# Tree-masked attention: stores moved from SyncE's hardware queue to GpSimd's software queue, behind the loads, with ten output buffers

## The chip, the cores and the metric

One NeuronCore of a Trainium2 chip. The metric is the device time of one execution in microseconds, median of several runs; lower is better. The profile's span is some 1.5 us shorter than that time. Engines are PE (TensorE), DVE (VectorE), ACT (ScalarE), POOL (GpSimd) and SP (SyncE). Sixteen DMA engines move the data, whichever of them issues it.

## The reference

Attention over 8 batches and 12 heads, 512 positions of 64 numbers, where a position sees only itself and its ancestors in a binary tree:

```python
mask[i, i] = 1
parent = i
while parent > 0:
    parent = (parent - 1) // 2
    mask[i, parent] = 1
scores = np.einsum('bhqd,bhkd->bhqk', Q, K) / np.sqrt(dim)
scores = scores + (1 - mask) * (-1e9)
weights = np.exp(scores - np.max(scores, axis=-1, keepdims=True))
weights = weights / (np.sum(weights, axis=-1, keepdims=True) + 1e-10)
return np.einsum('bhqk,bhkd->bhqd', weights, V)
```

Q, K, V and the result are 12.6 MB each in fp32: 37.7 MB are read, 12.6 MB written.

## The kernel before

It works on 48 pairs of heads, i = 0 to 47, six to a batch. For each: transposes of Q and K on PE (`tq`, `tk`), copies to `qt` (DVE) and `kt` (ACT), scores (`st`, `stx`), exponentials on ACT, values into `o`, then a reciprocal and a multiplication on DVE into `of`, which is stored. DVE also spreads each batch's V into `v` and `vx` ("copies"). The parts that matter:

```python
opool = ctx.enter_context(tc.tile_pool(name="opool", bufs=4))     # rec and of
...
def load(upto):                       # all loads that are due up to pair `upto`
    while plan and plan[-1][0] <= upto:
        _, src, b, h0, h1 = plan.pop()
        ...                           # 6 buffers each for Q, K and V of a batch
        nc.gpsimd.dma_start(          # fp32 -> bf16 on the way
            out=loaded[kind, b][:, h0:h1, :],
            in_=src[b, h0:h1].rearrange("h (p t) d -> p h (t d)", t=T),
        )
...
def values(i):
    ...
    nc.vector.tensor_tensor(out=of4, in0=o4[:, :, :, 0:D], in1=..., op=ALU.mult)
    nc.sync.dma_start(                # 128 partitions x 2 heads x 1 KB
        out=out[b, 2 * hp:2 * hp + 2].rearrange("h (p t) d -> p h (t d)", t=T),
        in_=of[:, :, :],
    )
...
for i in range(N):
    load(i + 9)
    if i + 2 < N:
        transposes(i + 2)
    if i + 1 < N:
        scores(i + 1)
    values(i)
    ...                               # a few of the copies of V
```

The order on PE, DVE, ACT and GpSimd is the program's order. DMAs issued on GpSimd share eight completion semaphores in turn, so each waits for the eighth before it.

The softmax here doesn't subtract the row's maximum and nothing guards it: scores larger than these inputs give would overflow.

## Time and profile before

| | before |
|---|---|
| time, median | 157.4 us |
| span in the profile | 156.0 us |
| busy: PE, DVE, ACT, POOL | 120, 103, 111, 49 us |
| loads on q0 / stores on q1 | 18.9 MB (bf16 side) / 12.6 MB and 0.5 MB of constants |

No compute engine is busy over 77% of the span, while the DMA engines are full until about 136 us. The prediction below shows the slices, the chain and the DMA queues, and reads them.

### The profile page before, as it was taken

The page shows a single profiled execution, that of the slowest core. Times are in us where ns is not written, and L with a number is a line of the kernel's source. Part 1 is how long each engine was busy: PE and PEld are TensorE (multiplying, and loading weights), DVE is VectorE, ACT ScalarE, POOL GpSimd, SP SyncE. Part 2 cuts the span into 40 slices and gives each one's busy share as a digit, 9 for nine tenths or more (in the row PEclk, how much of TensorE's full clock was granted, in tenths as well). Part 3 has the DMA queues.
Part 4 walks back from the last instruction along what each step waited for, and adds up shares of the span by engine and source line. Part 5 has one row for each costly group of instructions (what it writes and reads, how often), then busy time and mean ns, then how long its engine had stood idle before and what let it go on. Part 6 is the DMA issues. An engine that isn't in the chain of part 4 may idle for free.

```text
span 156.0 us, 5918 instructions
## 1 busy us (share of the span) xinstructions
PE 120.0 (77%) x2592; PEld 86.2 (55%) x2592; DVE 102.8 (66%) x243; ACT 111.0 (71%) x145; POOL 48.8 (31%) x65
## 2 busy tenths in 40 slices
PE   0539983966989897786998949986998659989950
PEld 0226752644667675564676627664676426767740
DVE  2119798097499876975589664986699635696541
ACT  3145792565799996985598937996899816999950
POOL 7974712333441323403432143503341130000000
PEclk9999999597799999999699977999999965999996
DMA  4999999999999999999999999999999999933432
GB/s 139 154 187 196 193 215 239 226 200 220 219 226 240 235 233 241 225 237 227 222 221 237 234 235 226 215 236 238 227 227 235 243 227 215 211 113 132 138 113 93
DMA packets 51210, 32.33 MB, mean 207 GB/s; under 512 B 1776, under 2 KB 51056, under 8 KB 51184
## 3 DMA queue, kind: packets, MB, share of 16 engines
q0 software_dynamic: 37840, 18.88, 89.6%
q1 hardware_dynamic: 13344, 13.08, 29.3%
q8 instruction: 20, 0.33, 0.8%
q14 instruction: 6, 0.05, 0.1%
HBM read 38.24 MB, written 12.58 MB: 326 GB/s over the span
## 4 chain that ended last, share of the span: by engine, by line
DMA 78%; PE 8%; DVE 4%; issue 3%; ACT 3%; POOL 2%; POOLq 0%
DMA ks<-in_K_dram 40%; DMA qs<-in_Q_dram 23%; DMA vs<-in_V_dram 15%; PE o L358 3%; DVE of L367 2%; PE st L311 2%; ACT etx L335 2%; PE stx L311 1%; POOL qs L222 1%; PE tk L275 1%; ACT kt L298 1%; PE tq L275 1%; DVE vx L261 1%; DVE rec L364 1%; ACT et L324 1%
## 5 line engine op out<-in xcount | busy, mean ns | idle before, releaser
L298 ACT COPY kt<-tk 128x512 bf16<-128x512 bf16 x48 | 28.2, 587 | 34.5 <-PE tk L275 33.9
L324 ACT ACTIVATE et<-st 128x1024 bf16<-128x1024 f32 x48 | 49.2, 1024 | 4.0 <-PE st L311 3.5
L358 PE MATMUL o<-v,et 128*64 128x65 bf16 (+1 forms) x576 | 39.0, 204 | 6.1 <-DVE v L261 4.8
L335 ACT ACTIVATE etx<-stx 128x768 bf16<-128x768 f32 x48 | 38.6, 804 | 0.0
L358 PE MATMUL o<-vx,etx 128*64 128x65 bf16 (+1 forms) x576 | 37.8, 200 | 0.8 <-issue 0.8
L358 PEld LDWEIGHTS <-et 128*64 128x64 bf16 (+1 forms) x576 | 28.9, 110 | 13.6 <-DVE v L261 5.9
L367 DVE TENSOR_TENSOR of<-o,rec 128x512 f32<-128x512 f32 x48 | 33.2, 691 | 1.7
L275 PE MATMUL tq<-ptile,qs 128*64 128x128 bf16 x384 | 21.6, 237 | 15.6 <-DMA qs<-in_Q_dram 10.1
L364 DVE RECIPROCAL rec<-o 128x8 f32<-128x8 f32 x48 | 9.8, 205 | 35.7 <-PE o L358 35.5
L222 POOL DMA_DIRECT2D qs<-in_Q_dram x26 | 20.3, 780 | 41.8 <-DMA vs<-in_V_dram 25.9
L358 PEld LDWEIGHTS <-etx 128*64 128x64 bf16 (+1 forms) x576 | 30.0, 111 | 0.4 <-issue 0.4
L261 DVE COPY vx<-vs 32x1536 bf16<-32x1536 bf16 (+3 forms) x54 | 28.8, 533 | 1.2
L222 POOL DMA_DIRECT2D ks<-in_K_dram x26 | 19.5, 750 | 30.7 <-DMA qs<-in_Q_dram 20.4
L275 PE MATMUL tk<-ptile,ks 128*64 128x128 bf16 x384 | 21.6, 238 | 8.4 <-DMA ks<-in_K_dram 8.1
L297 DVE COPY qt<-tq 128x512 bf16<-128x512 bf16 x48 | 19.9, 414 | 9.8 <-PE tq L275 9.3
L311 PEld LDWEIGHTS <-kt 64*128 64x128 bf16 x480 | 19.9, 102 | 11.4 <-issue 4.2
L275 PEld LDWEIGHTS <-qs 128*64 128x64 bf16 x384 | 15.2, 116 | 17.3 <-DMA qs<-in_Q_dram 10.6
L275 PEld LDWEIGHTS <-ks 128*64 128x64 bf16 x384 | 15.6, 121 | 10.7 <-DMA ks<-in_K_dram 9.4
L311 PE MATMUL st<-ctile 64*128 64x512 bf16 x96 | 20.3, 419 | 0.1
L311 PE MATMUL st<-qt,kt 64*128 64x512 bf16 x96 | 20.2, 417 | 0.1
L311 PE MATMUL stx<-qt,kt 64*128 64x96 bf16 x384 | 17.7, 215 | 0.5 <-issue 0.5
L311 PE MATMUL stx<-ctile 64*128 64x384 bf16 x96 | 17.3, 356 | 0.1
(11 smaller groups left out, 35.7 us busy)
## 6 DMA issues: line engine op xcount, KB each, us to landing
out_dram<-of SPq DMA_DIRECT2D x48, 256.0 KB, 6.2
qs<-in_Q_dram POOLq DMA_DIRECT2D x22, 256.0 KB, 19.1
ks<-in_K_dram POOLq DMA_DIRECT2D x22, 256.0 KB, 18.7
vs<-in_V_dram POOLq DMA_DIRECT2D x7, 768.0 KB, 22.4
vs<-in_V_dram POOLq DMA_DIRECT2D x2, 384.0 KB, 7.3
qs<-in_Q_dram POOLq DMA_DIRECT2D x4, 128.0 KB, 10.4
ks<-in_K_dram POOLq DMA_DIRECT2D x4, 128.0 KB, 10.0
ctile<-tree_codes SPq DMA_DIRECT2D x1, 288.0 KB, 3.1
```

The source lines that it names most:

```text
L222: nc.gpsimd.dma_start(out=loaded[kind, b][:, h0:h1, :], in_=src[b, h0:h1].rearrange("h (p t) d -> p h (t d)", t=T),)
L261: nc.vector.tensor_copy(out=o, in_=i)
L275: nc.tensor.matmul(out=o[D * hi:D * hi + D], rhs=perms[mat], lhsT=src[:, 2 * hp + hi, D * t:D * t + D], start=True, stop=True, is_transpos ...
L297: nc.vector.tensor_copy(out=qt[:, :], in_=tq[:, :])
L298: nc.scalar.copy(out=kt[:, :].rearrange("d (i j x) -> d i j x", j=2, x=32), in_=tk[:, :].rearrange("d (j i x) -> d i j x", j=2, x=32)[:, 0:8],
L311: nc.tensor.matmul(out=dst, lhsT=lhsT, rhs=rhs, start=first, stop=True, skip_group_check=not first,)
L324: nc.scalar.activation(out=et1[:, :, :], in_=st1[:, :, :], func=AF.Exp, scale=scale)
L335: nc.scalar.activation(out=etx[:, :, :, 32:P], in_=stx[:, :, 0:384].rearrange("p h (c q) -> p h c q", c=T), func=AF.Exp, scale=scale,)
L358: nc.tensor.matmul(out=o2[p0:p1, hi, (D + 1) * t:(D + 1) * (t + 1)], lhsT=e, rhs=v, start=kind == 0, stop=kind == 1,)
L364: nc.vector.reciprocal(out=rec[:, :, :, :], in_=o4[:, :, :, D:D + 1])
L367: nc.vector.tensor_tensor(out=of4, in0=o4[:, :, :, 0:D], in1=rec[:, :, :, :].to_broadcast([P, 2, T, D]), op=ALU.mult,)
```

## The change

Its intent: loads set the pace, and a store on a queue of its own takes its turns from them at once. Issued on GpSimd, behind the loads due nine pairs ahead, stores wait in the same ring until those loads have gone. Outputs then live longer, hence ten buffers. The last three stores have no load behind them and stay on SyncE.

```diff
-    opool = ctx.enter_context(tc.tile_pool(name="opool", bufs=4))
+    opool = ctx.enter_context(tc.tile_pool(name="opool", bufs=10))
...
-    state = {}
+    state, done = {}, {}
...
-        nc.sync.dma_start(
+        done[i] = of
+
+    def store(i):
+        b, hp = pairs[i]
+        eng = nc.gpsimd if i < N - 3 else nc.sync
+        eng.dma_start(
             out=out[b, 2 * hp:2 * hp + 2].rearrange(
                 "h (p t) d -> p h (t d)", t=T
             ),
-            in_=of[:, :, :],
+            in_=done.pop(i)[:, :, :],
         )
...
             load(i + 9)
+            if 0 < i < N - 2:
+                store(i - 1)
             if i + 2 < N:
                 transposes(i + 2)
             if i + 1 < N:
                 scores(i + 1)
             values(i)
+            if i >= N - 3:
+                store(i)
```

## The prediction

> **What bounds the kernel now.** I read the page's slices first, then the chain of work that ended last, then the waits, then the DMA view cut to stretches. The chain, first as shares of the span on the page, then as pieces in order of time (start, length, what):
>
> ```profile
> DMA 78%; PE 8%; DVE 4%; issue 3%; ACT 3%; POOL 2%; POOLq 0%
> ```
>
> ```profile
> 88.20 19.07 DMA qs<-in_Q_dram
> 107.28 0.28 issue
> 107.56 19.55 DMA ks<-in_K_dram
> 127.12 0.04 issue
> 127.16 0.64 PE tk L275 x8
> ```
>
> For 127 of 156 us the end hangs on one load behind another; from then on the chain is compute to the end. The load that hands over is K of heads 8 to 11 of batch 6. The first pair that needs it is pair 40 (pairs are counted 0 to 47), and its transposes are the ones at 127.16. The timeline of TensorE and VectorE shows that the last `of` of pair 47 ends at 152.66, so ten pairs' results (38 to 47) come in the 25.5 us after that landing: at first at half clock (the view of stretches has 0.50 for 127 to 133 us), later at 2.16 us a pair. This tail is compute, and the loads are ahead of it: the trace's last load lands at about 138 us, and pair 47's transposes are at 145.6.
>
> The page's slices and the DMA view say what the loads wait for. Whole span first, then 8 to 17 us (no store yet), 47 to 97 us (steady), and 0 to 125 us. Columns: packets, MB, time of the packets as a share of 16 engines.
>
> ```profile
> DMA  4999999999999999999999999999999999933432
> ```
>
> ```profile
> q0 software_dynamic: 3468, 1.72, 143.1%
> ```
>
> ```profile
> q0 software_dynamic: 13159, 6.57, 96.6%
> q1 hardware_dynamic: 5095, 4.91, 36.1%
> ```
>
> ```profile
> q0 software_dynamic: 34640, 17.31, 102.6%
> q1 hardware_dynamic: 10054, 9.91, 28.9%
> ```
>
> The engines are busy from 4 us to about 136 us. q0 carries the casting loads (1 KB fp32 in, 512 B bf16 out), q1 the stores (1 KB each). With the stores taken out, loads alone go at one packet per 42.9 ns and engine: 8 to 17 us is 9 us x 16 engines = 144 us of engine time for 1.72 MB / 512 B = 3,360 load packets. From 47 to 97 us there are 800 us of engine time for 6.57 MB / 512 B = 12,830 loads and 4.91 MB / 1,024 B = 4,795 stores; 12,830 x 42.9 ns = 550 us, the other 250 us are the stores': 52 ns each. A store of one head pair (256 KB, 16 packets per engine) thus costs 0.83 us of all 16 engines.
>
> **Does that add up to 127?** Before K of pair 40, each engine carries Q and K of 7 batches and V of 8: 14 x 96 + 8 x 96 = 2,112 packets, 17.30 MB in all; the view of 0 to 125 us has 17.31 MB, so the data are through at 125 and land 2 us later. 2,112 x 42.9 ns = 90.6 us. Stores by then: 9.91 MB less 0.49 MB of constants, 35.9 stores, x 0.83 us = 29.9 us. With 2.8 us until the first load has been issued and 2 us for landing the sum is 125.3; 1.8 us are left for the slow start and the constants. So the landing of that K, which sets the end, contains about 30 us of stores.
>
> **What the Trainium skill says.**
> - "DMA: Bandwidth & Descriptors", section "Queues, rings and completion order": each DMA engine takes turns between the queues that have work, and within a queue descriptors are taken in order. The trace agrees: a store issued on SyncE lands in a median of 6.2 us while loads issued before it take about 19 us, so a store on its own queue overtakes them.
> - Same page, "Anatomy of one DMA — SWDGE (gpsimd) path": the completion increment waits until the last byte is confirmed, longest for HBM, though the write of the semaphore itself is a tiny bubble. In the trace before, stores have their own queue, so whether such a completion holds up loads behind it in the same ring isn't shown.
> - "Advanced Engine Details and Errata", section "Clock Domains": an unobstructed 1 KiB descriptor takes 42 to 43 ns. The 42.9 ns of the loads agree with that; the 52 ns of the mixed stores lie above it.
> - "SBUF — State Buffer", section "SBUF: two separate sides": a DMA issued from GpSimd can starve for descriptors while VectorE holds the shared port in a fast mode. In the trace most descriptor runs are 0.70 to 0.85 us whatever VectorE does, the longest 1.22 us, so I give this little weight.
>
> **The change part by part.** The instruction order of the changed kernel shows PE, DVE and ACT unchanged; 45 store issues move from SyncE into GpSimd's stream, 3 stay.
>
> *What it reorders.* On GpSimd, store i-1 stands behind the loads due at iteration i, which run 9 pairs ahead. In one ring that is also the order of the transfers. Ahead of K of pair 40 stand stores 0 to 27, 28 of them, where the kernel before had moved 35.9. The total of bytes is the same; 7.9 stores go from before the landing that counts to after it.
> - At the old cost: 7.9 x 0.83 = 6.6 us earlier.
> - If a store packet in the same ring costs 47 ns, which is what store packets take when they have the engines alone (143 to 155 us: 37.5% of 12 us x 16 engines for 1.57 MB / 1,024 B = 1,533 packets): 28 x 16 x 47 ns = 21.1 us in place of 29.9, so 8.8 us earlier.
> - If it costs what a load costs, 42.9 ns: 19.2 us, so 10.7 us earlier.
> I take 8.8 us, because taking turns between two queues is the one thing that the mixed stretch has and the others don't, but I can't show that the 5 ns come from it.
>
> *What it costs GpSimd.* 45 more issues of about 0.75 us (the page's rows L222: 751 and 742 ns in the median) are 34 us on an engine that is busy 49 of 156 us. Per batch it issues 7 loads and 6 stores in 6 pairs x 2.7 us = 16 us, 1.25 us apiece. Beside the path.
>
> *What it adds as waits.* A GpSimd DMA reuses the semaphore of the eighth before it, so 8 are in flight: now some 4 loads and 4 stores (about 10 us of transfers) where it was 8 loads (19 us). A store also waits for its `of`. By the eighth-before rule, store 29 comes up when Q of pairs 38 and 39 has landed; compute is then near pair 34. So it has been ready for some 5 pairs, and the stream shouldn't stand.
>
> *The ten buffers.* `of` of pair j needs store j-10 landed. That store is right behind the loads of pair j+2 (for j = 6b+1, behind the next V as well), while `of` of j comes after the transposes of pair j+2 on PE anyway, about 3.7 us after their load's landing (127.1 to 130.8 in the chain). A store's 0.8 us and 2 us of landing fit in; behind a V (96 packets x 42.9 ns = 4.1 us) up to 2 us of wait may show, in a place where the next K isn't there yet.
>
> *Does the gain reach the end?* K of pair 40 lands at 127.1 - 8.8 = 118.3. The loads after it are 192 packets per engine (8.2 us) and 7 stores (5.3 us): the last lands at about 132, and pair 47 needs some 7 us more: 139. The compute tail from pair 40 ends at 118.3 + 25.5 = 143.8, so it still sets the end. The stores left at 132 are 13 x 0.75 = 10 us, done as their data come; the last is on SyncE, as before. Then 3.3 us from the last `of` to the end of the span, as before: span 147.2, and with the 1.35 us between the profile's span and the median time, **148.5 us**.
>
> **Rivals.**
> - *Store completions stall the ring.* If the increment after a write to HBM holds up the next load's data by 0.3 us or more, 28 stores cost 8.4 us and the gain is gone; at 0.5 us the kernel gets slower. For: stores that end alone take at least 2.1 us from issue to landing, for 0.75 us of data. Against: completion packets take 9 to 22 ns on either queue in the trace. It would make 155 to 162.
> - *GpSimd stands on a store whose pair isn't computed, and loads behind it come late.* Against: 5 pairs of slack above. For: the slack is counted on landings, and a slow stretch of compute would eat it. Some 150 to 153.
> - *One ring is better than two by more than the packets' time.* Then stores cost 43 ns or less, K of pair 40 lands at 116 and the time is 145 to 147. Compute stops it from going much lower: 48 pairs at some 2.35 us with spreading and a start of 15 us make an estimate of 128 to 130, plus the end.
> - *The time was hidden anyway* (compute the bound throughout). Against: the chain, and 34 us of idle ScalarE before its copy of K, released by `tk`. It would make 157.
>
> **Range and chances.** The sums at the three packet costs give 151, 148.5 and 146.5; waits move it up, a better ring down. Range 143.5 to 155. Faster by over 2% (under 154.2) needs only a third of the reckoned gain, so 0.77; within 2%, 0.16; slower, for a ring that stalls on completions, 0.07.
>
> **What would show it.** Right: the chain still hands over from a load of K to PE, at about 118 us; 28 stores, not 36, moved by then; the tail after it 25 us; DMA full to about 134 us with a higher sum in its last slices; loads land in some 10 us from issue, stores on GpSimd likewise; GpSimd's waits for VectorE near zero before the last loads. Wrong: long waits of GpSimd on `of`; VectorE idle before its multiplication, released by a store; slices of DMA below 9 in the middle; a rate per packet above 52 ns for stores. A chain that is PE, ACT or DVE from well before 110 us would mean that I have mistaken the bound after the change.

## The result, and the profile after

144.0 us in the median of four runs (143.25 to 145.38), against 157.37: the ratio is 0.916, with a 95% interval of 0.909 to 0.924. Ratios here are the mean time of one kernel's runs over that of the other's runs of the same rounds, so not quite the ratio of the medians quoted. Executions over 1.5% slower than the fastest of the same kernel are left out of the means. The result is correct. The time lies in the stated range, near its lower end; the gain is 13.4 us where 8.9 were reckoned.

The slices of the page of the changed kernel, in 40 parts of the span:

```profile
DMA  4999999999999999999999999999999999998343
GB/s 136 150 184 191 195 200 195 199 197 205 267 238 234 274 271 239 219 246 261 267 235 237 269 265 244 222 249 264 267 225 233 267 257 265 260 320 312 136 145 103
```

The DMA engines are as full as before. Until the tenth slice (35 us) there are almost only loads, near 197 GB/s; from then on, until about 124 us, 219 to 275 GB/s, where the kernel before had about 232 on average in its steady stretch. So it isn't only the order: in the same time more is moved. The same stretch as the prediction's, 47 to 97 us, from the DMA view of the changed kernel:

```profile
DMA packets 16163, 12.56 MB, mean 251 GB/s; under 512 B 662, under 2 KB 14907, under 8 KB 16151
q0 software_dynamic: 16151, 12.39, 134.0%
```

Loads (512 B), stores and completions are all on q0 now. About 1,244 packets lie between 2 and 8 KB: those are the stores, in packets of 4,096 B, four rows of 1 KB each. The packet records themselves carry 4,096 B 2,880 times, 45 stores x 64. So 5.10 MB are stores, and of the rest 14,245 packets are loads. With 42.9 ns for a load, as before: 800 us - 14,245 x 42.9 ns = 189 us for 1,244 store packets, 152 ns each, **38 ns per KB** where the mixed store of before cost 52. This takes for granted that loads cost the same beside stores as alone. A fit doesn't need that: take the packets that end in each of the 50 stretches of 1 us, and find the two costs that best fill the engines' 16 us of each (least squares). It gives 42 ns a load in both kernels, and 54 ns per KB of store before, 40 after.

Where stores stand in the ring, from the DMA view of 0 to 111 us (2 us before K of pair 40 lands, as 125 us was before):

```profile
DMA packets 36901, 25.36 MB, mean 228 GB/s; under 512 B 1315, under 2 KB 34939, under 8 KB 36882
q0 software_dynamic: 36594, 24.59, 132.3%
q1 hardware_dynamic: 288, 0.49, 1.4%
```

1,943 packets of 2 to 8 KB, less 128 of the constants, are 1,815 x 4 KB: 28.4 stores, for which the order of the stream promised 28, and 17.2 MB of loads. The semaphore events put that landing at 113.2 us: 13.9 us earlier than before.

But the chain of the profiled run doesn't lead to it any more. The chain on the page of the changed kernel:

```profile
DVE 38%; PE 33%; DMA 13%; issue 7%; ACT 4%; POOL 3%; POOLq 0%
PE o L358 13%; DVE vx L261 13%; DVE of L367 12%; DMA out_dram<-of 7%; PE st L311 6%; DMA ks<-in_K_dram 6%; DVE v L261 6%; PE tq L275 5%; PE stx L311 4%; DVE qt L297 4%; PE tk L275 4%; DVE rec L364 3%; ACT etx L335 2%; ACT kt L298 1%; POOL qs L222 1%
```

Loads have gone from 78% of the span to 6%, the K of the start. All else is PE and DVE taking turns. Pair 40's transposes start at 113.3 us, as soon as its K is there, without a noted wait: loads and compute are level. It is a close thing: in the profiles of e3 and e9 below, which change only where the rows go or which engine issues the last three stores, the chain still hands over from this K. The piece in e3:

```profile
103.77 10.42 DMA ks<-in_K_dram
```

The outputs come every 2.54 us from pair 0 (18.3) to pair 47 (137.7), never over 3.8 us apart, where before there were gaps of 6 or 7 us. The 7% that is `out_dram` are two pieces of 4.6 and 4.8 us that look like waits for a store's buffer and aren't: the view of waits lists no wait of DVE for a store, DVE's idle time in them (1.4 us at most) ends with `o` of PE, and e5 has such a piece of 6.2 us at 47 us, when its 18 buffers haven't all been used once.

One thing comes with the gain that no run here separates from it: the clock granted to TensorE. In the profile before its mean is 0.93, with 0.50 from 127 to 133 us, where the tail begins; in the changed kernel it is 0.99, and full but for the last slice. PE is busy 112 us for 120 with the same matmuls.

### The profile page after: what moved, and what is told of

Same layout as the page of the kernel before. It is cut to its first block, busy times and chain, and to the rows that moved or that the text cites. A ratio compares the mean times of both kernels' runs of the same rounds, so it can differ in the third digit from the quotient of the medians.

```text
span 141.5 us, 5912 instructions
## 1 busy us (share of the span) xinstructions
PE 112.2 (79%) x2592; PEld 82.5 (58%) x2592; DVE 104.1 (74%) x243; ACT 110.4 (78%) x145; POOL 83.0 (59%) x110
## 4 chain that ended last, share of the span: by engine, by line
DVE 38%; PE 33%; DMA 13%; issue 7%; ACT 4%; POOL 3%; POOLq 0%
PE o L358 13%; DVE vx L261 13%; DVE of L367 12%; DMA out_dram<-of 7%; PE st L311 6%; DMA ks<-in_K_dram 6%; DVE v L261 6%; PE tq L275 5%; PE stx L311 4%; DVE qt L297 4%; PE tk L275 4%; DVE rec L364 3%; ACT etx L335 2%; ACT kt L298 1%; POOL qs L222 1%
## 5 line engine op out<-in xcount | busy, mean ns | idle before, releaser
L324 ACT ACTIVATE et<-st 128x1024 bf16<-128x1024 f32 x48 | 49.2, 1024 | 1.8 <-PE st L311 1.1
L376 POOL DMA_DIRECT2D out_dram<-of x45 | 33.2, 739 | 27.1 <-DVE of L367 9.0
L358 PE MATMUL o<-v,et 128*64 128x65 bf16 (+1 forms) x576 | 37.3, 200 | 6.8 <-DVE v L261 5.4
L358 PE MATMUL o<-vx,etx 128*64 128x65 bf16 (+1 forms) x576 | 36.4, 195 | 1.7 <-issue 1.7
L358 PEld LDWEIGHTS <-et 128*64 128x64 bf16 (+1 forms) x576 | 27.6, 106 | 14.0 <-DVE v L261 6.6
L261 DVE COPY vx<-vs 32x1536 bf16<-32x1536 bf16 (+3 forms) x54 | 30.0, 556 | 1.2
L358 PEld LDWEIGHTS <-etx 128*64 128x64 bf16 (+1 forms) x576 | 28.5, 107 | 0.4 <-issue 0.4
L311 PEld LDWEIGHTS <-kt 64*128 64x128 bf16 x480 | 18.8, 96 | 9.1 <-issue 1.2
L364 DVE RECIPROCAL rec<-o 128x8 f32<-128x8 f32 x48 | 9.8, 204 | 19.0 <-PE o L358 18.3
L311 PE MATMUL st<-ctile 64*128 64x512 bf16 x96 | 19.2, 396 | 0.1
L311 PE MATMUL st<-qt,kt 64*128 64x512 bf16 x96 | 18.8, 386 | 0.1
L311 PEld LDWEIGHTS <-ctile 64*128 64x128 bf16 x192 | 10.4, 94 | 11.0 <-issue 1.4
```

Of the source, the lines that this page charges most:

```text
L261: nc.vector.tensor_copy(out=o, in_=i)
L311: nc.tensor.matmul(out=dst, lhsT=lhsT, rhs=rhs, start=first, stop=True, skip_group_check=not first,)
L324: nc.scalar.activation(out=et1[:, :, :], in_=st1[:, :, :], func=AF.Exp, scale=scale)
L358: nc.tensor.matmul(out=o2[p0:p1, hi, (D + 1) * t:(D + 1) * (t + 1)], lhsT=e, rhs=v, start=kind == 0, stop=kind == 1,)
L364: nc.vector.reciprocal(out=rec[:, :, :, :], in_=o4[:, :, :, D:D + 1])
L376: eng.dma_start(out=out[b, 2 * hp:2 * hp + 2].rearrange("h (p t) d -> p h (t d)", t=T), in_=done.pop(i)[:, :, :],)
```

## The experiments

Twelve kernels, in three groups, each group beside runs of the kernel before on the same chip (medians 156.9, 156.9 and 157.0 us). Where a kernel's numbers are wrong it is said.

### e1: compute without the loads

```diff
 (kernel before)
+            if b > 0:
+                loaded[kind, b] = loaded[kind, 0]
+                continue
```

> The kernel before, with only batch 0 of Q, K and V loaded and used for every batch (wrong result on purpose): compute and stores as they are, no loads to wait for after the first 10 us. It measures what compute alone takes. If the changed kernel (144.0 us) is bound by compute from about 20 us on, as its chain of waits says (DVE 38%, PE 33%, DMA 13%), this takes 138 to 143 us. If loads still set its end, as the prediction had it, compute alone is well below: the prediction's estimate for compute was 128 to 130 us plus the end, so about 132 us.

138.3 us (137.0 to 138.6; ratio 0.879). So compute alone, with its stores on SyncE, is 19 us below the kernel before and 5.7 us below the changed one. The prediction's estimate for it (about 132 with the end) was 6 us low: outputs come every 2.42 us, and the first at 17.6 us. Of the 19 us that loads cost before, the change has taken 13.

### e2: the order alone, on the old queue

```diff
 (changed kernel)
-    opool = ... bufs=10
+    opool = ... bufs=18
-        eng = nc.gpsimd if i < N - 3 else nc.sync
-        eng.dma_start(
+        nc.sync.dma_start(
...
-            if 0 < i < N - 2:
-                store(i - 1)
+            if i >= 8:
+                o = done[i - 8]
+                nc.gpsimd.tensor_copy(out=o[:, 0, 0:1], in_=o[:, 0, 0:1])
+                store(i - 8)
```

(and the last eight after the loop)

> The order alone: stores stay on SyncE's queue, but each is held back until GpSimd has issued the loads due 17 pairs ahead of it (a one-column copy on GpSimd in its place, 18 output buffers), so that about as many loads are moved ahead of each store as in the changed kernel. Store packets stay at 1 KB. Theory 'order': the gain is that stores stand behind loads, so this comes to 144 to 146 us. Theory 'packets': the software queue moves a store in 4 KB packets and so at less cost; then order alone gives the prediction's sum at the old cost, 150 to 152 us.

Median 150.3 us, but two of the four runs count as slow; the fast ones are 148.2 and 149.1, ratio 0.946 (0.936 to 0.957). That is 8.4 us from the order alone, about two thirds of the gain; the interval is 6.7 to 10.1 us. The old-cost sum of the prediction, 6.6 us, lies just under it; "order alone" as the whole cause (144 to 146 us) is refuted. The order was the intended one: in its DMA view of 0 to 119 us, 2 us before K of pair 40 lands, q1 has 7.57 MB, less the constants 27.0 stores. Its one profile is of a slow run, so I take from it no time, only what kind of thing the chain is:

```profile
DMA 71%; issue 10%; POOL 7%; DVE 4%; ACT 3%; PE 3%; POOLq 0%; DVEq 0%
```

Still loads: with stores at the old packet size, later stores alone don't free the kernel from its DMA engines.

### e3 and e4: rows that lie apart

Rows of the output are put 12 KB apart from partition to partition (wrong result), in the changed kernel and, as a control, in the kernel before:

```diff
-            out=out[b, 2 * hp:2 * hp + 2].rearrange(
-                "h (p t) d -> p h (t d)", t=T
-            ),
+            out=out[b].rearrange("h s d -> (h s d)").rearrange(
+                "(p h g x) -> g p h x", p=P, h=2, x=T * D
+            )[hp],
```

> The changed kernel, with each 1 KB row of the output put 12 KB from the row of the next partition (rows permuted, wrong result on purpose), so that the software queue cannot join four rows to one packet. Theory 'packets': store packets are 1 KB again, and the time goes to 147 to 151 us. Theory 'order': still 144 to 145 us.

> Control for the permuted output: the kernel before with the same permuted rows. Its store packets were 1 KB already, so both theories expect 157 us; a change of more than 1 us would mean that the place of the rows in HBM has a cost of its own, to be taken off e3.

e3 took 143.6 us (ratio 0.916), e4 157.35 (1.002). The control holds. But e3 didn't test what it was made for, as its DMA view of 47 to 97 us shows:

```profile
DMA packets 16027, 12.39 MB, mean 248 GB/s; under 512 B 650, under 2 KB 14798, under 8 KB 16017
q0 software_dynamic: 16017, 12.24, 133.7%
```

Still some 1,220 packets over 2 KB: the software queue makes 4 KB packets of four rows here too. So e3 can't speak for or against "packets". What it does show is that adjacent rows aren't needed for them.

### e5, e6 and e7: buffers, and GpSimd's waits

e5 is the changed kernel with `bufs=18`, e6 with `bufs=4`. e7 has 18 buffers and each store four pairs later:

```diff
-            if 0 < i < N - 2:
-                store(i - 1)
+            if 0 <= i - 5 < N - 3:
+                store(i - 5)
```

(with the two that remain, 43 and 44, after the loop)

> The changed kernel with 18 output buffers for ten. Its chain of waits has two pieces of over 4.5 us that are a store's transfer, each handing over to the next multiplication into an output tile. If the wait for a buffer's store is what keeps it 5.7 us above compute alone (138.3 us), this takes 139 to 142 us. If not, it stays at 143.5 to 144.5 us.

> The changed kernel with the four output buffers of before. The multiplication of pair j then needs the store of pair j-4, which stands in GpSimd's stream and in the ring behind the loads of about pair j+6. So compute can't come nearer than some six pairs to the last load, and after it (about 125 us) seven or eight pairs at 2.16 us remain: 146 to 151 us. If buffers don't matter (the wait of the 5.7 us lies elsewhere and stores land soon enough), 144 us.

> The changed kernel with each store four pairs later in GpSimd's stream (store i-5 at iteration i) and 18 buffers, so that GpSimd needn't wait for VectorE. In the changed kernel it waits some 22 us in all for outputs that aren't computed. If loads are held up by that (second rival of the prediction), this takes 140 to 142.5 us and less than e5. If the 5.7 us come from VectorE's copies being slowed while GpSimd writes descriptors, it stays at 143 to 144.5 us, and GpSimd's waits for VectorE are gone nevertheless.

**e5: 143.5 us, ratio 0.916**, the changed kernel's own. More than ten buffers bring nothing.

**e6: 157.5 us, ratio 0.997** (0.990 to 1.005; three of the six runs are slow, the fast ones took 155.3 to 157.4): with four buffers in place of ten the whole gain is gone. I had expected 146 to 151 and missed. The lines of its waits, and of its chain of waits from 24 to 42 us:

```profile
DVE of L367 <- DMA out_dram<-of: 15.1, 8, 9.6
```

```profile
25.42 0.10 issue
25.52 12.32 DMA out_dram<-of
37.84 0.03 issue
```

The multiplication of pair 4 needs the store of pair 0, which stands behind the loads of the first ten pairs: DVE holds still for 9.6 us, and PE behind it. My sum had only looked at the last load, and had left out this stop at the start.

**e7: 143.7 us, ratio 0.919**: nothing gained either. Here I had misread a view. By the view of waits, GpSimd in the changed kernel stands some 21 us on DVE, ahead of stores:

```profile
POOL out_dram L376 <- DVE of L367: 9.0, 7, 3.1
POOL out_dram L376 <- DVE v L261: 6.4, 2, 3.4
POOL out_dram L376 <- DVE rec L364: 4.0, 2, 3.1
```

One of them in the timeline of GpSimd, and the `of` that this store (pair 6) needs, in the timeline of DVE:

```profile
47.04 0.72 POOL L376 DMA_DIRECT2D out_dram<-of  x1 [3.35 <-DVE v L261]
```

```profile
35.95 0.69 DVE L367 TENSOR_TENSOR of<-o,rec 128x512 f32<-128x512 f32 x1
```

The output had been ready for ten microseconds. A store waits for two things, its output and the eighth DMA before it, and the view names whichever event came last by its own reckoning. The eighth before it is the V that was issued at 35.54; by the semaphore events it landed at 46.5. That is the real wait, and in e7, where outputs are older still, the view lists waits of the same length. It costs nothing: other DMAs are in the ring meanwhile, and the slices stay full.

### e8: what 45 descriptor runs on GpSimd do to DVE

The edit of e1 (only batch 0 loaded) on the changed kernel.

> The changed kernel with only batch 0 loaded (wrong result on purpose): as e1 (138.3 us), but with the 45 stores on GpSimd. If GpSimd's 45 descriptor runs slow VectorE's copies, VectorE is busy 1.5 to 3 us longer than in e1 (99.5 us) and the time is 139 to 141 us; if they don't, 138 us. The rest of the 5.7 us would then be the loads' share.

141.1 us (ratio 0.898) against e1's 138.3 (0.879): with no loads in the way in either, stores on GpSimd cost compute 2.8 us. DVE is busy 104.1 us against 99.5: 4.6 more, where I had expected 1.5 to 3. Groups of DVE by form, e1 and then e8; count, busy us and mean ns of one:

```profile
L264 DVE COPY v<-vs 32x768 bf16<-32x768 bf16 x28 | 9.8, 351 | 0.6
L264 DVE COPY vx<-vs 32x1536 bf16<-32x1536 bf16 x28 | 15.4, 551 | 0.6
L264 DVE COPY vx<-vs 64x1536 bf16<-64x1536 bf16 x14 | 7.8, 556 | 0.3
```

```profile
L264 DVE COPY v<-vs 32x768 bf16<-32x768 bf16 x28 | 13.1, 468 | 0.6
L264 DVE COPY vx<-vs 32x1536 bf16<-32x1536 bf16 x28 | 15.4, 551 | 0.6
L264 DVE COPY vx<-vs 64x1536 bf16<-64x1536 bf16 x14 | 9.4, 668 | 0.3
```

Only copies of V grew, and not all of them; `qt`, which is copied out of PSUM, and the multiplications have the same means. They grew where they begin within a descriptor run of GpSimd. From e8's timeline of DVE, a copy that was under way when a run began, the next one, which grew, and one that had all but ended when its run began, with GpSimd's runs:

```profile
61.39 0.55 DVE L264 COPY vx<-vs 32x1536 bf16<-32x1536 bf16 x1
61.95 0.58 DVE L264 COPY v<-vs 32x768 bf16<-32x768 bf16 x1
...
73.98 0.35 DVE L264 COPY v<-vs 32x768 bf16<-32x768 bf16 x1
```

```profile
61.66 0.72 POOL L379 DMA_DIRECT2D out_dram<-of  x1 [1.44 <-DVE of L370]
...
74.25 0.80 POOL L379 DMA_DIRECT2D out_dram<-of  x1 [1.61 <-DVE of L370]
```

Taken over the whole trace of the changed kernel: of the 28 copies into `v` of 32x768, 20 overlap a descriptor run in time and take 437 ns on average, 8 don't and take 350, none over 352; of the 42 into `vx` of 1,536 columns, 32 overlap and take 625 ns, 10 don't and take 552. In e1 none overlaps, and the means are 351 and 553. But overlap alone doesn't stretch a copy. In e8 75 copies overlap a run, and 24 of them grow, by 70 to 240 ns: those that begin 0.29 to 0.47 us after the run's start, and each takes as long as if it had stood still until 0.53 us after it. The other 51, all 26 of 32x1536 among them, begin by 0.10 us after it at the latest and take their usual time, within 4 ns. So in this trace it counts where in a run a copy begins. DVE pays 4.6 us for it, and as DVE is a link of the chain, 2.8 us reach the end. The kernel before paid some of it too, for its 61 load issues: DVE was busy 102.8 us there, but it had time to spare.

The rest of the gap, 144.0 - 141.1 = 2.9 us, comes with the loads, their transfers or their 51 further issues on GpSimd; which wait it is I haven't isolated.

### e9: the last three stores

```diff
-        eng = nc.gpsimd if i < N - 3 else nc.sync
+        eng = nc.gpsimd
```

> The changed kernel with the last three stores on GpSimd too, as the others. A store on GpSimd in a quiet stretch lands in 2.6 us where one on SyncE takes 2.1 us (e8), and its issue of 0.73 us stands in for 0.37 us: the last one ends about 1 us later, 144.5 to 145.5 us. If the three on SyncE make no difference, 144.0 us.

145.1 us, ratio 0.925 (0.920 to 0.929) against 0.916 (0.909 to 0.924): about 1.3 us later, as expected, though the intervals overlap.

### e11 and e12: is it the packet or the ring?

e11 is the kernel before with 2 KB to a partition's store (rows permuted, wrong); e12 is the changed kernel with bf16 output tiles that the store casts (correct within the tolerance).

```diff
 (e11, kernel before)
-                "h (p t) d -> p h (t d)", t=T
-            ),
+                "h s d -> (h s d)").rearrange("(p h x) -> p h x", p=P, h=2),
 (e12, changed kernel)
-        of = opool.tile([P, 2, T * D], fp32)
+        of = opool.tile([P, 2, T * D], bf16 if i < N - 3 else fp32, name=...)
```

> The kernel before with its two 1 KB pieces of a store put side by side in HBM (rows permuted, wrong result on purpose), so that a store on SyncE's queue has packets of 2 KB. A store packet of 1 KB costs 52 ns of an engine there, one of 4 KB in the software ring 38 ns per KB. If the size of the packet makes that difference, 2 KB packets cost some 45 ns per KB or less, K of pair 40 lands 4 us or more earlier and the time is 151 to 153.5 us. If taking turns between two queues makes it, this stays at 156 to 157.5 us.

> The changed kernel with output tiles in bf16 but for the last three, cast to fp32 by the stores. Casting loads aren't gathered to 4 KB packets in this ring, so casting stores shouldn't be either: 1 KB written per packet, in one ring with the loads. If packets of 4 KB make stores cheap, a store packet costs about 50 ns again, and the time goes to 146 to 149 us; if it is enough to be in one ring, a packet costs 43 ns or less and the time stays at 143.5 to 145 us.

e11: 152.9 us, ratio 0.972 (0.966 to 0.978). The DMA view of e11, 47 to 97 us:

```profile
q0 software_dynamic: 14355, 7.18, 106.0%
q1 hardware_dynamic: 2546, 4.63, 28.0%
```

7.18 MB / 512 B = 14,023 loads x 42.9 ns = 602 us; 4.63 MB / 2,048 B = 2,261 stores take the other 198 us, 88 ns each or 44 ns per KB. On the same queue, in the same order, the same bytes: larger packets alone cut a store from 52 to 44 ns per KB, and the time by 4.1 us; K of pair 40 lands at 123.1 us, 4.0 earlier. As other places of the rows alone change nothing (e4), that settles that packet size counts.

e12: 147.9 us, ratio 0.942. The time is what "packets" expected, the rate isn't. The DMA view of e12, same stretch:

```profile
DMA packets 19584, 12.29 MB, mean 246 GB/s; under 512 B 646, under 2 KB 19574, under 8 KB 19574
q0 software_dynamic: 19574, 12.14, 156.6%
```

No packets over 2 KB. 12.14 MB in 18,928 packets of 512 and 1,024 B are 14,145 loads and 4,783 stores, so (800 - 607) us / 4,783 = 40 ns a store packet of 1 KB. That is near the 38 of the changed kernel, and far from 52. (The fit by stretches of 1 us has 46 ns per KB in e11 and 43 in e12, between 54 before and 40 in the changed kernel; a load stays at 42.) So in one ring with the loads even small packets are cheap; though these read only 512 B from SBUF each, which no other run does. By 28 stores x 16 KB an engine x 2 ns the rate accounts for 1 us of the 3.9 us that e12 loses. Its K of pair 40 lands at 116.1 us, 2.9 later than in the changed kernel, and why is not shown; stores' transfers are 15% of its chain, but its view of waits has no wait of DVE for a store. Either change by itself, larger packets in two queues or one ring with small packets, brings more than half of the 14 ns between 52 and 38; how they divide when both are there stays open.

### e13: fewer, larger stores

Stores of two pairs in one DMA, as an attempt to better the change: half the descriptor runs, the same bytes.

```diff
+            if i % 2 == 0:
+                done[i] = done[i + 1] = opool.tile([P, 4, T * D], fp32, name="ofs", bufs=6)
+            of = done[i][:, 2 * (i % 2):2 * (i % 2) + 2, :]
...
-            if 0 < i < N - 2:
-                store(i - 1)
+            if i % 2 and 0 < i - 2 < N - 4:
+                store(i - 3)
```

(the last four pairs each with a buffer of its own, stored on SyncE)

> The changed kernel with stores of two head pairs (four heads, 512 KB) in one DMA, six such output buffers, and the last four pairs stored one by one on SyncE: 22 descriptor runs on GpSimd for 45. Bytes and order are nearly the same. If VectorE's copies lose 4.6 us to GpSimd's descriptor runs (99.5 us busy in e1, 104.1 in e8 and in the changed kernel), and that loss goes by the number of runs, VectorE's busy time falls by 1.5 to 2.5 us and the time to 141.5 to 143 us. If it goes by the number of descriptors, nothing changes: 144 us.

145.6 us in the median, three of the six runs slow; fast ones 143.5 to 145.3, ratio 0.920 (0.914 to 0.926). No gain. GpSimd is busy 67 us for 83, but DVE 103.6 for 104.1 (the profile is of a slow run): fewer runs don't give DVE its time back, which fits a loss by descriptors rather than by runs, without proving it. No run here beats the changed kernel clearly; e5 is its equal.

## Why the prediction was right, and where it was off

- **The bound before: right.** The chain, the sum to 127 us, and e1 (138.3 us without loads) say the same: loads cost 19 us.
- **The order: right.** 28.4 stores were moved by 111 us where 28 were foretold, and the order by itself gave 8.4 us (e2; reckoned at the old cost: 6.6).
- **The cost of a store in the ring: the term that was mis-sized.** "If a store packet in the same ring costs 47 ns" stood for the middle of the range. It costs 38 ns per KB, in packets of four rows and without a second queue beside it; which of the two does how much is open. 28 stores x 16 x 38 ns = 17.0 us stand in place of 21.1; the K of pair 40 landed at 113.2 and not at 118.3. Put into the prediction's own sum, 17.0 us would have given 114.2 for that landing and 144.4 for the time, so this one term is nearly all of the miss of 4.5 us. The 47 ns were also misread: they are the mean length of a packet's record, and by the same measure the loads of 8 to 17 us take 59 ns (143.1% of 144 us for 3,468 packets), though one passes every 42.9. The two kinds of number can't be set side by side. The rival "one ring is better than two by more than the packets' time" is what happened, to its stated 145 to 147 and a little beyond.
- **"The compute tail from pair 40 ... still sets the end": right in size, half right as a picture.** From that landing to the last output were 25.2 us, where 25.5 were foretold, so the sum comes out. But in the profiled run PE didn't wait for that load. The prediction named the sign of this itself, a chain of PE, DVE and ACT from well before 110 us, and it came: the chain is compute from 13 us on, but for the two pieces that aren't waits. In e3 and e9 it still hands over from that K. So loads and compute have become level, which the prediction didn't foresee.
- **The floor of compute: estimated too low**, at about 132 us; it is 138.3 with the stores on SyncE and 141.1 with them on GpSimd. It was no term of the sum; but it leaves the loads only 2.9 us to gain in the changed kernel, where the estimate had left 12.
- **"I give this little weight" (the shared port): wrong engine.** GpSimd's 45 runs for stores indeed stay short (0.72 to 0.92 us, median 0.73). It is DVE that is held up, for 4.6 us, of which 2.8 reach the end (e8 against e1); that the port does it isn't shown. This is part of what the change costs, and wasn't in the sum.
- **Ten buffers: right.** The view of waits has none of DVE for a store, e5 is no faster, and e6 shows that four would have undone everything.
- **GpSimd standing on uncomputed outputs: rightly ruled out** (e7), though its view of waits looks like it.

So the time was right to about 3%, and 144.0 lies only 0.5 us inside the range: the mechanism (loads first, stores later) held, one cost was set too high, and the bound after the change was only half seen.

## What to carry to other kernels

Where the DMA engines set the pace, ask of each store both when it takes its place among the loads, and in what packets and beside which other queue it travels; here the first was worth some 8 of 13 us and the second, by what the rates say, most of the other 5, and both only with enough output buffers to let stores be late. When the DMA engines have been freed, look for the next bound before reckoning further: a run with the loads left out gives its floor. And when a view names an engine that had long been done, count back to the DMA whose semaphore is reused.

## What the Trainium skill lacked or had wrong

- "DMA: Bandwidth & Descriptors", "Issuing engines are not separate DMA queues", says that spreading issues over engines saves only the sequencer's time. Here the issuing engine also decided the packets (1 KB on SyncE's queue, 4 KB on GpSimd's) and whether stores share the loads' ring, and a store cost the DMA engines 52 against 38 ns per KB. Packets count in this: 2 KB on SyncE's queue cost 44 (e11).
- The same page gives a packet in the software queue as up to 4096 B preferably ("SWDGE vs HWDGE vs iDMA"). That agrees (2,880 packets of 4,096 B). It doesn't say that rows need not be adjacent (e3: 12 KB apart), nor that casting DMAs aren't gathered (loads at 512 B; stores of e12 at 1 KB).
- "Perfetto Trace Analysis", "DMA Optimizations", suggests one issuing engine for inputs and another for outputs. In this kernel the opposite is faster by 8.4%, as long as the ring's order is the wanted one and outputs have buffers for it.
- "SBUF — State Buffer", "SBUF: two separate sides": its box warns of GpSimd's descriptors waiting for DVE, though its text says that whichever starts first, a GpSimd op or a DVE op in a two-port mode, holds the shared ports for the whole instruction. Here the loss showed on DVE (busy 4.6 us longer in e8 than in e1), and not for whole runs: runs took 0.72 to 0.80 us, and only copies that began 0.29 to 0.47 us after a run's start were held, until 0.53 us after it. Copies that were under way were not held, which agrees. That the shared ports are what held them is not shown.
